# Prompt attention: the third head's near scores on 160 keys per 32 successive queries, and no cache copy behind the 30th weight load

## The chip, the cores and the metric

The kernel runs on one core of one Trainium2 chip. The metric is the time of one execution on the device in microseconds (us), as the median of several runs. A separate execution is profiled; every row shown below comes from that one.

A core has TensorE (PE in the profile; PEld is its loading of weights), VectorE (DVE), ScalarE (ACT), GpSimd (POOL) and SyncE (SP), which here only issues DMAs. Each engine works off its own list of instructions in order, and semaphores tie the lists together. Matmul results arrive in PSUM; everything else lies in SBUF or in HBM.

## The reference

One layer of a decoder is computed for a prompt of 256 tokens and for 8 x 4 sample tokens that share the weights. The part that matters here is the attention of the prompt:

```python
GROUPS = ((128, 1), (512, 4), (2048, 16))     # window, dilation
...
valid = (du >= 0) & (du <= BAND) & (uk >= 0)
bias = slopes[:, None, None] * (dil * du).astype(jnp.float32)[None]
sc = jnp.einsum('nrbqhd,nrbkhd->nrbhqk', qb, kw).astype(jnp.float32) * ATT_SCALE - bias
sc = jnp.where(valid[None, None, :, None], sc, -jnp.inf)
m = jnp.max(sc, axis=-1, keepdims=True)
p = jnp.exp(sc - m)
den = jnp.sum(p, axis=-1, keepdims=True)
```

There are four heads in each of three groups. In group 0 (dilation 1, "near") a query sees its own key and the 128 before it. In groups 1 and 2 (dilations 4 and 16, "far") it sees every fourth or sixteenth key. The three groups' results of a head are merged by their softmax denominators, which comes to one softmax over the scores of all three groups. Around this stand a combined input projection, a gated convolution, an output projection, a feed-forward block with a convolution, and two layer norms; and the caches of the sample tokens are copied from inputs to outputs.

## The kernel before, in words

**Weight blocks.** All dense work is a list of 313 blocks of weights (`weight_list`), each of 128 output features by up to 2048 inputs, behind three blocks that are handled apart. `prepare` (from L196) loads a block into a tile `wst` (three buffers) with a DMA on SyncE's queue, and splits each half of it into a high part `whi` (ScalarE copies, L265) and the rest `wlo` (VectorE subtracts, L265); there are four buffers of halves. `product` takes a block and runs three matmuls for each 128 inputs: `whi` by the high part of x, `whi` by its rest, `wlo` by the high part. Behind the loads with numbers from 20 on that end in 0, 3 or 7, `prepare` calls `copy_rest`, which issues one DMA of the list `copies`: 84 copies of a megabyte from HBM to HBM, the sample caches on their way to the outputs (L163). The list is used from its end, one copy at each such load, so a skipped place shifts all later copies to the next places.

**Order.** The program is written as one sequence, and a planner with a simulated timeline puts each engine's instructions in order before anything runs. `behind` adds an order without a wait; `in_a_row` chains instructions.

**The prompt's attention.** The q blocks come first, then the k and v blocks of the four heads, three of each to a head. Once the third head's are through, `three_heads` (from L579) is started; it is a generator that is advanced behind each following `product`, so that its work lies beside the products of the fourth head. Its steps:

- `score_row` (from L483) issues the score matmuls of three heads in one row, ahead of the next product. For each head, half of the queries (h = 0, 1) and group, four matmuls with 32 queries each (c = 0 to 3) run on the four column strips of TensorE. For the far groups a matmul takes the 32 queries and the keys of one class (positions with the same remainder by 4). For the near group with h = 1 there are two ways, chosen by `in_time(j)`, which is false for `FIRST_HEAD` = 2, the third head, alone:
  - queries in order of time, 32 successive ones to a matmul, which together see only 160 keys (`NB_W`);
  - queries by class, each matmul with all 256 keys.
- The softmax works on rows by class. So scores by time have to be moved: `later_near` (L523) copies them out of PSUM into the tile `by_time`, shifted by 32 columns per strip (four copies of 32x160, on ScalarE, L531), and `by_class_rows` (L533) regroups the rows with four DMAs of SyncE's queue (L537) into the scores' tile `s_half[1]`.
- `softmax(j)` first calls `scored`, six VectorE instructions that add the distance penalties to the scores (L543; the last of them the near group of h = 1, from `s_half[1]` or, for the third head, straight from PSUM), then for each half a maximum, an exponential on ScalarE and a scaling (L554 to L558).
- `weights` transposes the probabilities in blocks of 32 on VectorE (L464) and moves the blocks to their places with ScalarE and GpSimd copies (L472, L468); the ScalarE copies are issued a few to a product, from the list `soon`.
- The heads go in the order third, first, second. With each, the next head's `later_near` is called right after `softmax`, and its `by_class_rows` after `weights`, as there is one `by_time` and one set of `s_half`.

When the fourth head's k and v are through, its own `score_row` also issues `output_row` (from L439, its matmuls L452): the matmuls of the first, second and third head's probabilities with their values, 48 instructions for each head, in that order.

**The penalties.** `load_distances` loads the distances between queries and keys: for h = 0 in four DMAs (one to each class) into one tile `m_first` that holds all groups, for h = 1 in eight, near and far apart.

Of the kernel before, what the change touches and what calls it, by code (L numbers as in the profile page):

```python
# [17 lines left out]
P = 128  # L18
# [35 lines left out]
FIRST_HEAD = 2  # L54
# [34 lines left out]
N_LATE = 3  # L89
N_PAUSE = 5  # L90
# [19 lines left out]
def layer_kernel(ctx: ExitStack, tc: tile.TileContext, ins, outs):  # L110
# [85 lines left out]
    def prepare():  # L196
# [13 lines left out]
        if n >= 20 and n % 10 in (0, 3, 7):  # L210
            copy_rest(d)
# [151 lines left out]
    m_first = pa_take(NG * P).rearrange("p (g k) -> p g k", g=NG)  # L363
    m_near = [m_first[:, 0], pa_take(2 * P)]
    m_all = [m_first[:, 1:], pa_take((NG - 1) * 2 * P).rearrange("p (g k) -> p g k", g=NG - 1)]
# [34 lines left out]
    def load_distances(h):  # L400
# [3 lines left out]
        for c in range(NC):  # L404
            at = slice(c * NW, (c + 1) * NW)
            if h:
                behind(sp.dma_start(m_near[h][at], m[c, :, 0]), w_load[0])
                behind(sp.dma_start(m_all[h][at], m[c, :, 1:]), w_load[0])
            else:
                behind(sp.dma_start(m_first[at], m[c]), w_load[0])  # L410
# [69 lines left out]
    def in_time(j):  # L480
        return j != FIRST_HEAD

    def score_row(heads):  # L483
# [5 lines left out]
        for n, (j, kT, k_class) in enumerate(heads):  # L489
# [49 lines left out]
    def scored(j, s3):  # L539
        s = s_half  # L540
        for h, g in ((0, 0), (0, 1), (0, 2), (1, 1), (1, 2), (1, 0)):
# [3 lines left out]
                s[h][:, at] if h and not g and in_time(j) else s3[h][g],  # L545
# [3 lines left out]
    def softmax(j, s3):  # L549
        s = s_half  # L550
        scored(j, s3)
        for h in range(2):
            st = sb(wk, [P, 4], "st", bufs=4)
            dve.reduce_max(st[:, 0:1], s[h], AX.X)  # L554
            dve.tensor_scalar_mul(st[:, 1:2], st[:, 0:1], -SCALE)
            act.activation(s[h], s[h], AF.Exp, bias=st[:, 1:2], scale=SCALE, accum_out=st[:, 2:3])
            dve.reciprocal(st[:, 3:4], st[:, 2:3])
            dve.tensor_scalar_mul(s[h], s[h], st[:, 3:4])  # L558
# [20 lines left out]
    def three_heads(heads, vT):  # L579
# [935 lines left out]
```

## Time and profile before

| what | value |
|---|---|
| median of 3 runs | 1701.38 us (1700.85 to 1701.54) |
| the profiled execution | 1701.37 us, of which its span is 1699.6 us |
| granted clock of TensorE in it | 0.999 |
| VectorE busy in the span | 1200.9 us |
| SyncE's queue (q1) | 430.54 MB, 69.2% of 16 DMA engines' span |
| row of score matmuls of three heads | 181.9 to 184.8 us |
| row of score and output matmuls with the fourth head | 221.0 to 225.3 us |

How to read the rows below. Times are us from the start of the span, unless marked ns. A row of the timeline is: start, duration (of all that is merged in the row), engine, line of the kernel, operation, written tile <- read tiles, shape, how many; in brackets the idle time of the engine just before, and what ended it. A row of the waits is: who waited <- for whom, us in total, times, longest. A row of the windows is: the stretch, its length, then for PE, PEld, DVE, ACT and POOL the busy time and (x) the number of instructions, then the granted clock, the share of the DMA engines and GB/s. "issue" is a wait for nothing that the profile shows. The matmuls in f32 that belong to the scores are two instructions each; a row of 8 is a set of four.

### The profile page before, as it was taken

The page shows a single profiled execution, that of the slowest core. Times are in us where ns is not written, and L with a number is a line of the kernel's source. Part 1 is how long each engine was busy: PE and PEld are TensorE (multiplying, and loading weights), DVE is VectorE, ACT ScalarE, POOL GpSimd, SP SyncE. Part 2 cuts the span into 40 slices and gives each one's busy share as a digit, 9 for nine tenths or more (in the row PEclk, how much of TensorE's full clock was granted, in tenths as well). Part 3 has the DMA queues.
Part 4 walks back from the last instruction along what each step waited for, and adds up shares of the span by engine and source line. Part 5 has one row for each costly group of instructions (what it writes and reads, how often), then busy time and mean ns, then how long its engine had stood idle before and what let it go on. Part 6 is the DMA issues. An engine that isn't in the chain of part 4 may idle for free.

```text
span 1699.6 us, 34341 instructions
## 1 busy us (share of the span) xinstructions
PE 1692.0 (100%) x14094; PEld 1689.4 (99%) x14094; DVE 1200.9 (71%) x1553; ACT 944.9 (56%) x1694; POOL 396.2 (23%) x529
## 2 busy tenths in 40 slices
PE   9999999999999999999999999999999999999998
PEld 9999999999999999999999999999999999999998
DVE  6477789889887767655888886776554555555576
ACT  6477796665666655544546664555433454445455
POOL 0123232223332221110454440111100010011175
PEclk9999999999999999999999999999999999999999
DMA  9788778676678888577766668666666666767553
GB/s 322 265 304 347 281 285 321 241 251 245 250 293 314 336 303 337 210 261 255 282 236 223 223 216 322 224 255 226 229 239 224 223 228 246 294 223 251 199 174 112
DMA packets 61918, 436.57 MB, mean 257 GB/s; under 512 B 8064, under 2 KB 12288, under 8 KB 24064
## 3 DMA queue, kind: packets, MB, share of 16 engines
q1 hardware_dynamic: 60464, 430.54, 69.2%
q10 hardware_dynamic: 1296, 3.83, 0.6%
q8 instruction: 110, 1.80, 0.4%
q14 instruction: 48, 0.39, 0.1%
HBM read 427.50 MB, written 94.53 MB: 307 GB/s over the span
## 4 chain that ended last, share of the span: by engine, by line
PE 99%; DVE 0%; DMA 0%; issue 0%; ACT 0%; ACTq 0%; DVEq 0%
PE acc L259 32%; PE acc L261 32%; PE acc L260 32%; PE acc L344 1%; PE acc L452 0%; DMA yah<-in_x 0%; DVE acc L1186 0%; PE att L507 0%; PE acc L507 0%; DVE yah L1186 0%; PE acc L1175 0%; PE acc L1172 0%; PE acc L1171 0%; PE att L1090 0%; ACT yah L1196 0%
## 5 line engine op out<-in xcount | busy, mean ns | idle before, releaser
L265 DVE TENSOR_TENSOR wlo<-wst,whi 128x1024 fp32r<-128x1024 f32 (+1 forms) x579 | 746.6, 1292 | 388.0 <-ACT whi L265 383.7
L265 ACT CAST whi<-wst 128x1024 fp32r<-128x1024 f32 (+1 forms) x579 | 588.8, 1020 | 648.9 <-PE acc L260 578.8
L261 PE MATMUL acc<-xh,wlo 128*128 128x288 f32 (+1 forms) x3216 | 920.0, 286 | 0.6 <-issue 0.6
L259 PE MATMUL acc<-xh,whi 128*128 128x288 f32 (+1 forms) x3216 | 920.3, 286 | 0.0
L260 PE MATMUL acc<-xl,whi 128*128 128x288 f32 (+1 forms) x3216 | 920.0, 286 | 0.0
L259 PEld LDWEIGHTS acc<-xh,whi 128*128 128x128 f32 x3216 | 607.8, 189 | 1.2 <-issue 1.1
L260 PEld LDWEIGHTS acc<-xl,whi 128*128 128x128 f32 x3216 | 607.8, 189 | 0.0
L261 PEld LDWEIGHTS acc<-xh,wlo 128*128 128x128 f32 x3216 | 607.8, 189 | 0.0
L260 PE MATMUL acc<-yal,whi 128*128 128x288 f32 x1216 | 347.5, 286 | 0.0
L261 PE MATMUL acc<-yah,wlo 128*128 128x288 f32 x1216 | 347.4, 286 | 0.0
L259 PE MATMUL acc<-yah,whi 128*128 128x288 f32 x1216 | 347.2, 286 | 0.0
L260 PEld LDWEIGHTS acc<-yal,whi 128*128 128x128 f32 x1216 | 229.8, 189 | 0.0
L261 PEld LDWEIGHTS acc<-yah,wlo 128*128 128x128 f32 x1216 | 229.7, 189 | 0.0
L259 PEld LDWEIGHTS acc<-yah,whi 128*128 128x128 f32 x1216 | 229.6, 189 | 0.0
L955 POOL COPY qk_s<-u 128x2 f32<-128x2 f32 x44 | 37.2, 845 | 534.5 <-ACT u L1274 487.1
L943 DVE SCALAR_TENSOR_TENSOR cy<-u,prm,cy 128x304 f32<-128x304 f32 x120 | 71.1, 593 | 6.2 <-ACT cy L941 3.5
L656 POOL TENSOR_TENSOR cache<-cache,cst 128x1024 f32<-128x1024 f32 x16 | 35.4, 2216 | 109.4 <-DMA cache<-in_cv 103.6
L656 POOL TENSOR_TENSOR cache<-cache,qk_s 128x1024 f32<-128x1024 f32 x16 | 32.9, 2058 | 66.1 <-DMA cache<-in_ck 56.5
L966 DVE TENSOR_TENSOR ya<-cy,acc 128x256 f32<-128x256 f32 x104 | 27.7, 310 | 26.6 <-PE acc L261 26.0
L265 ACT CAST yah<-ya 128x288 fp32r<-128x288 f32 x76 | 32.6, 429 | 22.6 <-DVE ya L966 13.6
L654 ACT ACTIVATE cache<-cache,qk_s 128x128 f32<-128x128 f32 x128 | 40.6, 393 | 0.0
L654 ACT ACTIVATE cache<-cache,cst 128x128 f32<-128x128 f32 x128 | 40.0, 391 | 0.0
(288 smaller groups left out, 1187.5 us busy)
## 6 DMA issues: line engine op xcount, KB each, us to landing
wst<-in_w_in SPq DMA_DIRECT2D x112, 1024.0 KB, 5.2
wst<-in_w_up SPq DMA_DIRECT2D x88, 1024.0 KB, 4.9
cache<-in_ck SPq DMA_DIRECT2D x18, 1024.0 KB, 8.0
cache<-in_cv SPq DMA_DIRECT2D x18, 1024.0 KB, 7.7
wst<-in_w_a SPq DMA_DIRECT2D x16, 1024.0 KB, 5.0
wst<-in_w_out SPq DMA_DIRECT2D x16, 1024.0 KB, 4.9
wst<-in_w_down SPq DMA_DIRECT2D x32, 512.0 KB, 4.5
wst<-in_w_down SPq DMA_DIRECT2D x16, 1024.0 KB, 4.8
```

What stands on the lines that cost most here:

```text
L259: pe.matmul(out, hi[:, c, :], xh_k, start=k == 0, stop=False)
L260: pe.matmul(out, hi[:, c, :], xl_k, start=False, stop=False)
L261: last_mm[0] = pe.matmul(out, lo[:, c, :], xh_k, start=False, stop=k == nk - 1)
L265: return act.copy(hi, src), dve.tensor_tensor(lo, src, f32(hi), ALU.subtract)
L344: i = pe.matmul(o[b], first_w(term == 2, b, k), xk, start=k == 0 and term == 0, stop=k == KD - 1 and term == 2,)
L654: behind(act.activation(o[:, a, b], t[:, a, b], AF.Copy, scale=w[:, a, b : b + 1]), w_split[0])
L656: behind(pool.tensor_tensor(o, t, w.unsqueeze(3).broadcast_to([P, *n]), ALU.mult), w_split[1])
L943: dve.scalar_tensor_tensor(y, u[:, i : i + YW], prm[:, w0 + i : w0 + i + 1], y, ALU.mult, ALU.add)
L955: pool.tensor_copy(dst[:, 0:2], u[:, SEQ : SEQ + 2])
L966: dve.tensor_tensor(a, b, c, ALU.mult)
```

## The change

It has three parts.

1. The third head's near scores of h = 1 are computed by time, as the other heads' are: `in_time` goes, all heads take 160 keys per 32 successive queries. The third head's q of the near group is therefore copied in two pieces instead of one. The scores go the way of `later_near` and `by_class_rows`.
2. The order in `three_heads` follows from that. `scored` and `softmax` are split: `EARLY` are the scores that are there without regrouping (h = 0, and the far groups of h = 1), `LATE` is the near group of h = 1; `softmax(h)` does one half. The third head's `later_near` and `by_class_rows` are called right behind `score_row`; its early scores and first half follow, and its late scores and second half come one product later, ahead of `weights`. The first head's `later_near` is called after the third head's `weights`, and no longer beside its softmax.
3. `prepare` leaves out the copy behind load 30 (`N_SCORES`). The distances of h = 0 are loaded like those of h = 1, near and far in tiles of their own, with eight DMAs.

```diff
-FIRST_HEAD = 2
+EARLY, LATE = ((0, 0), (0, 1), (0, 2), (1, 1), (1, 2)), ((1, 0),)
...
+N_SCORES = 30
...
-        if n >= 20 and n % 10 in (0, 3, 7):
+        if n >= 20 and n % 10 in (0, 3, 7) and n != N_SCORES:
             copy_rest(d)
...
-    m_first = pa_take(NG * P).rearrange("p (g k) -> p g k", g=NG)
-    m_near = [m_first[:, 0], pa_take(2 * P)]
-    m_all = [m_first[:, 1:], pa_take((NG - 1) * 2 * P).rearrange("p (g k) -> p g k", g=NG - 1)]
+    m_near = [pa_take((1 + h) * P) for h in range(2)]
+    m_all = [pa_take((NG - 1) * (1 + h) * P).rearrange("p (g k) -> p g k", g=NG - 1) for h in range(2)]
...
-            if h:
-                behind(sp.dma_start(m_near[h][at], m[c, :, 0]), w_load[0])
-                behind(sp.dma_start(m_all[h][at], m[c, :, 1:]), w_load[0])
-            else:
-                behind(sp.dma_start(m_first[at], m[c]), w_load[0])
+            behind(sp.dma_start(m_near[h][at], m[c, :, 0]), w_load[0])
+            behind(sp.dma_start(m_all[h][at], m[c, :, 1:]), w_load[0])
...
-                [second[:, far_keys(1, g) if g else slice(0, NB_W if in_time(j) else 2 * P)] for g in range(NG)],
+                [second[:, far_keys(1, g) if g else slice(0, NB_W)] for g in range(NG)],
...
-                        elif h and in_time(j):
+                        elif h:
                             k = kT[:, c * NW : c * NW + NB_W]
                         else:
-                            k = kT[:, : (1 + h) * P]
+                            k = kT[:, :P]
...
-    def scored(j, s3):
+    def scored(j, s3, parts):
         s = s_half
-        for h, g in ((0, 0), (0, 1), (0, 2), (1, 1), (1, 2), (1, 0)):
+        for h, g in parts:
...
-        order = FIRST_HEAD, 0, 1
+        order = 2, 0, 1
+        later_near(s3[order[0]])
+        by_class_rows()
         for n, j in enumerate(order):
-            softmax(j, s3[j])
-            if n < 2:
-                later_near(s3[order[n + 1]])
+            scored(j, s3[j], EARLY)
+            softmax(0)
+            if n:
+                scored(j, s3[j], LATE)
+                softmax(1)
+            if n == 1:
+                later_near(s3[order[2]])
             yield 1
+            if n == 0:
+                scored(j, s3[j], LATE)
+                softmax(1)
             weights(p_three[j])
+            if n == 0:
+                later_near(s3[order[1]])
             no_keys()
             if n < 2:
                 by_class_rows()
...
-        softmax(head[0], s3[0])
+        scored(head[0], s3[0], EARLY + LATE)
+        softmax(0)
+        softmax(1)
...
-            n = SEQ if g or not in_time(j) else P
+            n = SEQ if g else P
```

More of the change, by code (lines that the diff above doesn't have):

```diff
@@ L478, in moved @@
                 move((a, b), out[b : b + 32, :, a : a + 32], src[a : a + 32, :, b : b + 32], on_dve)
-    def in_time(j):
-        return j != FIRST_HEAD
     def score_row(heads):
@@ L544, in scored, with softmax @@
                 s[h][:, at], m_far[:, h, g - 1, : (1 + h) * NW] if g else m_near[h], -SLOPE[g][j] / SCALE,
-                s[h][:, at] if h and not g and in_time(j) else s3[h][g],
+                s[h][:, at] if h and not g else s3[h][g],
                 ALU.mult, ALU.add,
             )
-    def softmax(j, s3):
+    def softmax(h):
         s = s_half
[L551 to L558, printed above, removed]
+        st = sb(wk, [P, 4], "st", bufs=4)
+        dve.reduce_max(st[:, 0:1], s[h], AX.X)
+        dve.tensor_scalar_mul(st[:, 1:2], st[:, 0:1], -SCALE)
+        act.activation(s[h], s[h], AF.Exp, bias=st[:, 1:2], scale=SCALE, accum_out=st[:, 2:3])
+        dve.reciprocal(st[:, 3:4], st[:, 2:3])
+        dve.tensor_scalar_mul(s[h], s[h], st[:, 3:4])
     def values(vT):
```

## The prediction

> **What bounds the kernel now.** I read the page first, for the share of each engine and for the number of instruction pages.
>
> ```profile
> span 1699.6 us, 34341 instructions
> PE 1692.0 (100%) x14094; PEld 1689.4 (99%) x14094; DVE 1200.9 (71%) x1553; ACT 944.9 (56%) x1694; POOL 396.2 (23%) x529
> ...
> q8 instruction: 110, 1.80, 0.4%
> ```
>
> TensorE is busy for 1692.0 of 1699.6 us; no other engine comes near. So an edit can win time only by taking work from TensorE or by closing one of its gaps, and it can lose time only by opening a gap. I therefore asked next what TensorE waits for, in the view of waits filtered to it, which has these three lines and no more:
>
> ```profile
> PE acc L275 <- PEq L1502: 0.8, 1, 0.8
> PE acc L344 <- ACT xh L316: 0.7, 1, 0.7
> PE acc L261 <- issue: 0.6, 1, 0.6
> ```
>
> The first two are the start of the kernel, before anything that is edited. The third is the only stall in the body. The timeline of TensorE has it at 188.3 us, 3.5 us behind the row of score matmuls that the change edits:
>
> ```profile
> 188.16 0.29 PE L259 MATMUL acc<-xh,whi 128*128 128x288 f32 x1
> 188.28 0.29 PE L260 MATMUL acc<-xl,whi 128*128 128x288 f32 x1
> 189.17 0.28 PE L261 MATMUL acc<-xh,wlo 128*128 128x288 f32 x1 [0.60 <-issue]
> ```
>
> Two matmuls that otherwise follow each other by 0.12 us (188.16 and 188.28) are 0.89 us apart, so the stall costs 0.77 us. "issue" says that no semaphore that the profile knows ended it. The stretches around it, and two answers of the DMA view (for 173.3 to 188.3 us and for 186.4 to 188.3 us), suggest a cause:
>
> ```profile
> 173.00:181.90 8.90, 8.90 (x74) 8.78 (x72) 5.17 (x5) 5.94 (x13) 0.44 (x1) 1.00 0.95 333
> 181.90:184.80 2.90, 2.90 (x146) 2.58 (x145) 2.09 (x4) 2.40 (x6) 1.70 (x5) 1.00 1.01 411
> 184.80:188.30 3.50, 3.50 (x32) 3.50 (x30) 2.94 (x13) 0.89 (x4) 1.37 (x4) 1.00 1.01 413
> ```
>
> ```profile
> q8 instruction: 1, 0.02, 0.5%
> ```
>
> ```profile
> q8 instruction: 1, 0.02, 3.6%
> ```
>
> TensorE runs 2 x 14094 = 28188 instructions and queue 8 carries 110 packets: 256 instructions to a packet, so queue 8 is TensorE's program. Between 173 and 188.3 us TensorE used 146 + 291 + 62 = 499 instructions, nearly two packets' worth, because the score row alone takes 291 in 2.9 us. In that time only one packet came, and it came after 186.4 us. At the usual pace of one packet per 256 instructions it was due when 256 - 146 = 110 of the row's 291 instructions were through, at about 183 us. So the program itself was about 3.5 us late, while the DMA engines were fully taken (shares 0.95, 1.01 and 1.01 in the rows). That the stall is this late packet is my reading; no row names it.
>
> **The change, part by part.** (1) The third head's near scores of the second half: four matmuls of 256 columns become four of 160. The timeline has both shapes:
>
> ```profile
> 183.13 0.46 PE L507 MATMUL long<-dd,yah 128*32 128x160 f32 x8
> 183.41 0.41 PE L507 MATMUL long<-cy,yah 128*32 128x64 f32 x16
> ...
> 183.97 0.62 PE L507 MATMUL acc<-dd,yah 128*32 128x256 f32 x8
> 184.41 0.41 PE L507 MATMUL acc<-yal,yah 128*32 128x64 f32 x16
> ```
>
> From start to start the 160-column group takes 0.28 us and the 256-column group 0.44 us. The change takes 0.16 us from TensorE and leaves its number of instructions as it is.
>
> (2) The copy behind load 30 goes. In the trace it is this one (behind it on the same queue a cache load and the next weight loads; rows of SyncE's DMA lines with their time to landing):
>
> ```profile
> L163 SPq DMA_DIRECT2D out_o_ck<-in_ck x1: 793/793/793, 172.9 to 172.9; - x1
> ...
> DMA to landing us min/median/max: 9.5/9.5/9.5
> ```
>
> ```profile
> L821 SPq DMA_DIRECT2D cache<-in_ck x1: 531/531/531, 173.8 to 173.8; - x1
> ...
> DMA to landing us min/median/max: 12.2/12.2/12.2
> ```
>
> The copy lands at 172.9 + 9.5 = 182.4, the cache load at 173.8 + 12.2 = 186.0: the queue is served in order, at about 3.6 us a megabyte here. The late packet of instructions started just behind that landing. Without the copy the cache load lands near 182.4 and everything behind it some 3 to 3.6 us sooner, so at 183 us one transfer less stands ahead of the packet. To spare TensorE the stall it must come 0.77 us sooner. Bounds for this term: nothing (the packet is as late as now) and 0.77 us (the stall is gone). I take 0.77, since 3 us of backlog vanish where 0.8 are needed.
>
> The list of copies is only shifted, so one more copy runs at the end, behind load 300 at about 1606 us. It is a megabyte like the others, and the weights behind it have time:
>
> ```profile
> wst<-in_w_down SPq DMA_DIRECT2D x16, 768.0 KB, 4.4
> ```
>
> ```profile
> 1611.29 54.91 SPq L207 DMA_DIRECT2D wst<-in_w_down  x13
> ```
>
> ```profile
> 1622.73 1.05 ACT L265 CAST whi<-wst 128x1024 fp32r<-128x1024 f32 x1
> ```
>
> The load issued at 1611.29 is first read at 1622.73, 11.4 us later, and such loads land after 4.4 us (the DMA view's row). A whole 3.6 us of copy ahead of it still fits. I cost it at nothing; without that cover it would be at most 3.6 us.
>
> (3) The distances of the first half come in eight DMAs, not four, and the q copy of the third head is two ScalarE copies of 128 columns, not one of 256. Four more issues of 0.41 us (row below) hold SyncE's queue for 1.6 us at 27 us, ahead of a weight load; the q copy adds one ScalarE instruction, of some 0.3 us by the copies in part 4 (1.21 us for four). TensorE shows no wait there now, so nothing; the bound is 1.6 us, if that load were already the last thing that TensorE waits for.
>
> ```profile
> L410 SPq DMA_DIRECT2D yal<-in_cst x4: 382/410/421, 26.0 to 27.3; - x4
> ```
>
> (4) The third head, which is first in the softmax order, now takes the way of the others: four ScalarE copies to the buffer by time, four DMAs that regroup it by class, and only then the last scores and the second softmax. The rows of these in before (ScalarE, VectorE, SyncE, and the chain that ended last):
>
> ```profile
> 183.67 1.21 ACT L531 COPY yal<-att 32x160 f32<-32x160 f32 x4 [0.41 <-ACT dd L910]
> ...
> 191.57 1.05 ACT L265 CAST whi<-wst 128x1024 fp32r<-128x1024 f32 x1 [1.95 <-PE acc L260]
> ...
> 219.79 1.32 ACT L472 COPY yah<-yah 32x160 f32<-32x160 f32 x4
> ```
>
> ```profile
> 189.37 0.85 DVE L464 STREAM_TRANSPOSE yah<-yal 128x640 f32<-128x640 f32 x1
> ...
> 195.34 0.42 DVE L543 SCALAR_TENSOR_TENSOR yal<-yal 128x256 f32<-128x256 f32 x1 [1.13 <-DMA yal<-yal]
> ...
> 204.89 0.84 DVE L464 STREAM_TRANSPOSE yah<-yal 128x640 f32<-128x640 f32 x1
> ...
> 210.05 0.43 DVE L543 SCALAR_TENSOR_TENSOR yal<-yal 128x256 f32<-128x256 f32 x1
> ...
> 214.39 0.85 DVE L464 STREAM_TRANSPOSE yah<-yal 128x640 f32<-128x640 f32 x1
> ```
>
> ```profile
> 190.29 3.72 SPq L537 DMA_DIRECT2D yal<-yal  x4
> 194.11 0.53 SPq L207 DMA_DIRECT2D wst<-in_w_in  x1
> 194.69 0.56 SPq L163 DMA_DIRECT2D out_o_cv<-in_cv  x1
> ```
>
> ```profile
> 222.04 3.29 PE acc L452 x144
> ```
>
> The four copies cost ScalarE 1.21 us, the DMAs 3.72 us of SyncE's queue at a time (185 to 190 us) in which it has nothing else to issue. Scores are done at about 184.4, copied at 185.7, and then the four DMAs: now it takes from their first issue at 190.29 to the last scores at 195.34, 5.1 us, so the third head's last scores start at 185.7 + 5.1 = 190.8. From the last scores to the end of the transposition the second head needs 210.05 to 215.24, 5.2 us. So its transposition ends at 190.8 + 5.2 = 196.0 and not at 190.2: 5.8 us later. The next head's regrouping starts from there, and with 5.1 us more its last scores start at 201.1. If the load and the copy of 194.11 and 194.69 stand in front, it is up to 202.6. So the last scores of the first head come 5.8 to 7.3 us late. But between those scores and the end of that head's transposition pass now 10.4 us (195.34 to 205.73) where the bare chain needs 5.2; VectorE fills the rest with moves of values that can as well run while it waits. So 0.6 to 2.1 us of lateness are left for the second head, whose last moves end at 219.79 + 1.32 = 221.1 now, and then at 221.7 to 223.2.
>
> Who waits for them is TensorE's output row at 222.04, of 3.29 us for three heads, one after the other: the second head's weights are read from 222.04 + 1.1 = 223.1, and with TensorE 0.9 us ahead of now from 222.2. So the chain ends between 0.5 us ahead of its time and 1.0 us behind it. Bounds: nothing below (this chain cannot give TensorE anything), and 7.3 - 1.1 = 6.2 us above, if VectorE's other work does not move into the wait. I take nothing, the end at which the count without the copy in front arrives; the rest is the second rival.
>
> **Sum.** 0.16 from the columns and 0.77 from the stall, nothing from the rest: 0.93 us less. The profiled execution took 1701.37 us (1699.6 of span and 1.8 around it), the median is 1701.38, so the two need no correction: 1701.4 - 0.9 = 1700.5 us, 0.05% faster, which is no change by the measure of 0.2% (3.4 us), about what a measurement of this kernel can tell from no change.
>
> **Rivals.** *The stall stays.* The packet of instructions comes as late as now, because the loads that move up take the place of the copy: DMA shares stay near 1.0 until 188 us. For it: three more megabytes stand in the queue. Against it: 3 us less ahead of the packet. Time: 1701.37 - 0.16 = 1701.2 us. A page of the Trainium skill would have it so: "DMA: Bandwidth & Descriptors", section "Queues, rings and completion order", says that each DMA engine goes round its queues packet by packet, so that a fetch on its own queue would not stand behind whole transfers of another. The landing at 186.0 and the fetch just after it speak against it, though not for certain. "Runtime: NRT & Kernel Launch", section "Instruction fetch mechanics", has programs fetched in blocks of 256 instructions, as counted here, but gives TensorE room for 2048; with that much, 499 instructions could not starve it, and the stall would be something else and stay. By either rule the sum is 1701.2.
>
> *The regrouping comes late and TensorE waits at its output row* (the slower side). The mechanism is the chain of part 4: one more DMA round trip ahead of two others, with the copy of 194.69 in front of the second. It decides from about 1.1 us of lateness at the second head's last moves (222.2 - 221.1). Price: lateness less 1.1 us; at 2 us of lateness it takes back the gain (1701.3), at 4 us it is 1703.3, at the full 7.3 us 1706.6. For it: by the count above there is hardly any slack. Against it: the 5.2 us of other work in that chain, which the count moves only as far as the wait is long.
>
> *Weights come late* because VectorE, waiting in order for a DMA, holds back a weight rest: it needs a wait of more than 2 us more than now at one place. ScalarE's casts in this stretch wait for TensorE to free a buffer (1.95 us at 191.57), so the weights are ahead. Price: what the wait exceeds 2 us by; 1702 to 1704 us for 1.5 to 3.5 us.
>
> **How the numbers follow.** Forecast (columns and stall) 0.45; stall stays 0.2; late regrouping 0.27, of which 0.05 beyond 3.4 us; late weights 0.06; anything faster by over 3.4 us 0.02, since only 7.6 us of the span are not TensorE's, most of them at its two ends. Range: from 1700.0, the forecast less half the spread of the runs, to 1703.0, which takes in the stall that stays and the late regrouping up to 3.6 us of lateness; beyond it stand about 0.15. Faster by over 0.2%: 0.02; within: 0.92; slower: 0.06.
>
> **What would show it.** Right: the group of the third head's near matmuls is 0.28 us long; no "issue" line near 188 us, and queue 8's packet before 185.9 us; the cache load of 173 us lands near 182.4; no wait of TensorE at the output row (L452 in before). Wrong: a gap of TensorE at 222 us that ends on ScalarE, GpSimd or a transposition; a gap between 185 and 221 us that ends on a weight rest; a stall "issue" as long as before.

## The result and the profile after

| | before | after |
|---|---|---|
| median (8 runs each, side by side) | 1701.31 us (1700.75 to 1701.54) | 1705.72 us (1704.04 to 1707.27) |
| ratio after : before | | 1.0026, 95% interval 1.0017 to 1.0036 |
| the profiled execution, its span | 1701.37, 1699.6 us | 1704.78, 1703.0 us |

The changed kernel is slower by 4.4 us in the medians and by 3.4 us in the two profiled executions (the profile before has a stall of 0.77 us in it that not every execution has, as the last experiment shows). That lies outside the predicted range (1700.0 to 1703.0). The second rival came true, and a part of the third with it.

The view of waits, filtered to TensorE, of the kernel after (who waited <- for whom, us in total, times, longest):

```profile
PE acc L449 <- ACT yah L469: 2.8, 1, 2.8
PE acc L262 <- DVE wlo L266: 0.9, 1, 0.9
PE acc L276 <- PEq L1507: 0.8, 1, 0.8
```

The third line was there before. The "issue" line is gone, as predicted; the first two lines are new. TensorE's timeline shows where they are (start, duration, line, tiles, form; in brackets the idle time before the row and what ended it):

```profile
183.16 0.46 PE L501 MATMUL long<-dd,yah 128*32 128x160 f32 x8
183.43 0.41 PE L501 MATMUL long<-cy,yah 128*32 128x64 f32 x16
...
184.00 0.46 PE L501 MATMUL acc<-dd,yah 128*32 128x160 f32 x8
184.27 0.41 PE L501 MATMUL acc<-yal,yah 128*32 128x64 f32 x16
...
220.98 1.28 PE L449 MATMUL acc<-yah,yal 128*32 128x256 f32 x48
225.08 1.30 PE L449 MATMUL acc<-yah,yal 128*32 128x256 f32 x48 [2.82 <-ACT yah L469]
...
251.16 0.29 PE L261 MATMUL acc<-xl,whi 128*128 128x288 f32 x1
252.31 0.39 PE L262 MATMUL acc<-xh,wlo 128*128 128x288 f32 x1 [0.87 <-DVE wlo L266]
```

The third head's near group takes 0.27 us from start to start (184.00 to 184.27) where it took 0.44. But the output row stops between the first head's 48 matmuls and the second head's: these start at 225.08, where 222.1 was due (220.98 and the 1.1 us that 48 matmuls take). The last matmul before the gap starts at 221.99, so the gap is 3.09 us from start to start; the same step took 0.09 us before (222.86 to 222.95). The matmul at 252.31 comes 1.15 us after its neighbour, 1.03 too late, and the next one 0.11 more (at 252.54).

The bookkeeping from the start of the score row (181.93 before, 181.95 after) to the last matmul (1693.61 and 1696.91), in us: columns -0.16, stall at 188.3 -0.77, wait in the output row +3.00, the rest of the row of the fourth head's scores and the outputs +0.05, weight rest +1.14: +3.26. Measured: 1511.68 us before, 1514.96 after, +3.28. (The first output matmul starts at 221.85 in before, 39.92 us behind the score row; the prediction's 222.04 is where the chain view begins to count that row.)

Behind the wait stand VectorE, ScalarE and SyncE's queue (the timeline of each; compare the transpositions at 189.37, 204.89 and 214.39 before):

```profile
192.35 0.42 DVE L537 SCALAR_TENSOR_TENSOR yal<-yal 128x256 f32<-128x256 f32 x1 [2.32 <-DMA yal<-yal]
...
196.43 0.85 DVE L461 STREAM_TRANSPOSE yah<-yal 128x640 f32<-128x640 f32 x1
...
203.12 2.90 DVE L467 COPY yah<-yal 32x192 f32<-32x192 f32 x11
...
206.14 0.40 DVE L537 SCALAR_TENSOR_TENSOR yal<-yal 128x256 f32<-128x256 f32 x1
...
210.31 0.85 DVE L461 STREAM_TRANSPOSE yah<-yal 128x640 f32<-128x640 f32 x1
...
220.06 0.85 DVE L461 STREAM_TRANSPOSE yah<-yal 128x640 f32<-128x640 f32 x1
```

```profile
184.80 1.21 ACT L525 COPY yal<-acc 32x160 f32<-32x160 f32 x4 [1.52 <-PE acc L501]
...
222.62 2.32 ACT L469 COPY yah<-yah 32x160 f32<-32x160 f32 x7
```

```profile
178.38 6.21 SPq L208 DMA_DIRECT2D wst<-in_w_in  x2
186.03 2.45 SPq L531 DMA_DIRECT2D yal<-yal  x4
195.89 0.33 SPq L208 DMA_DIRECT2D wst<-in_w_in  x1
196.27 0.56 SPq L164 DMA_DIRECT2D out_o_ck<-in_ck  x1
197.30 2.41 SPq L531 DMA_DIRECT2D yal<-yal  x4
```

| what | before | after | later by |
|---|---|---|---|
| third head's transposition, start | 189.37 | 196.43 | 7.06 |
| first head's, start | 204.89 | 210.31 | 5.42 |
| second head's, start | 214.39 | 220.06 | 5.67 |
| second head's last ScalarE move, end | 221.11 | 224.94 | 3.83 |

The copies at 203.12 are the moves of the third head's values: `values` transposes them, `moved` puts the blocks in their places, with 12 copies on VectorE. So 7.06 us of lateness came in with the third head, and 3.83 us of it reached the moves that the output row waits for. The predicted price was lateness less 1.1 us: 2.7 us; the trace has 2.82.

### The profile page after: what moved, and what is told of

The parts are those of the page before. It is cut to its first block, busy times and chain, and to the rows that moved or that the text cites. A ratio compares the mean times of both kernels' runs of the same rounds, so it can differ in the third digit from the quotient of the medians.

```text
span 1703.0 us, 34360 instructions
## 1 busy us (share of the span) xinstructions
PE 1692.9 (99%) x14094; PEld 1690.2 (99%) x14094; DVE 1198.9 (70%) x1553; ACT 946.1 (56%) x1699; POOL 396.7 (23%) x529
## 3 DMA queue, kind: packets, MB, share of 16 engines
q10 hardware_dynamic: 1296, 3.83, 0.6%
## 4 chain that ended last, share of the span: by engine, by line
PE 97%; DMA 1%; ACT 1%; DVE 0%; issue 0%; SPq 0%; ACTq 0%; DVEq 0%
PE acc L262 32%; PE acc L260 32%; PE acc L261 32%; PE acc L345 1%; DMA out_o_k<-dd 1%; DMA yal<-yal 0%; PE acc L276 0%; ACT whi L266 0%; DVE wlo L266 0%; ACT cache L659 0%; ACT dd L469 0%; PE att L501 0%; PE acc L1180 0%; PE acc L1177 0%; PE acc L1176 0%
```

## The experiments

All ratios are to the kernel before on the same chip. Its median was 1701.21 us beside the two runs with the copy behind load 30, the one with a transfer less and the one with the output row later; 1700.96 beside the third head from PSUM, the detour alone, the values early and the first head's regrouping early; 1701.13 beside the last three versions. The intervals reach about 0.1% (1.7 us) to each side, so differences of under 2 us between two versions are read from the traces here and not from the medians.

### Which part costs the time

**The copy alone.** The kernel before, without the copy behind load 30:

```diff
-        if n >= 20 and n % 10 in (0, 3, 7):
+        if n >= 20 and n % 10 in (0, 3, 7) and n != 30:
```

> The kernel before, with only the copy behind load 30 left out. Theory (the stall of 0.77 us near 188 us is the late packet of TensorE's program, held up by the DMA backlog): the line 'issue' near 188 us is gone, queue 8's packet starts before 185.9 us, no new wait: 1700.5 us. Rival (the stall has another cause, and in the changed kernel it went with the new order): the stall stays, 1701.3 us.

Measured: 1701.13 us (1700.66 to 1701.33), ratio 0.9997 (0.9988 to 1.0006). In its trace the stall is gone, and from the score row's start to the last matmul 0.8 us are gone too; in the medians 0.1 us is left, so the time is nearer to the rival's than to the theory's. Why, is taken up with the last experiment.

**The copy put back.** The kernel after, with the copy behind load 30:

```diff
-        if n >= 20 and n % 10 in (0, 3, 7) and n != N_SCORES:
+        if n >= 20 and n % 10 in (0, 3, 7):
```

> The changed kernel with the copy behind load 30 kept. Theory (the regrouping DMAs wait in SyncE's queue behind what was issued before them): the third head's regrouping lands about 3 us later than at 192.2 us, the output row's wait of 2.8 us grows by 1 to 3 us, and the stall of 0.8 us near 188 us is back: 1707 to 1710 us. Rival (the chain is as long as it is, whatever lies in the queue): only the 0.8 us come back, 1706.5 us.

Measured: 1706.54 us (1705.68 to 1708.03), ratio 1.0029 (1.0019 to 1.0040). Two lines of TensorE's waits:

```profile
PE acc L449 <- ACT yah L469: 2.8, 1, 2.8
...
PE acc L262 <- issue: 0.5, 1, 0.5
```

The stall is back, and the wait at the output row is the same to 0.01 us (2.82), as the rival had it. The third head's regrouping lands at 192.6 to 193.5 us instead of 191.8 to 192.2, not 3 us later. So the copy has nothing to do with that wait.

**The third head straight from PSUM again**, the rest of the diff kept (order, distances, copy):

```diff
-                [second[:, far_keys(1, g) if g else slice(0, NB_W)] for g in range(NG)],
+                [second[:, far_keys(1, g) if g else slice(0, NB_W if j != 2 else 2 * P)] for g in range(NG)],
...
-                        elif h:
+                        elif h and j != 2:
...
-                            k = kT[:, :P]
+                            k = kT[:, : (1 + h) * P]
...
-                s[h][:, at] if h and not g else s3[h][g],
+                s[h][:, at] if h and not g and j != 2 else s3[h][g],
...
-        later_near(s3[order[0]])
-        by_class_rows()
...
-            n = SEQ if g else P
+            n = SEQ if g or j == 2 else P
```

> The changed kernel with the third head's near scores by class and on 256 columns again, read straight from PSUM; the split softmax, the order of calls, the distances' DMAs and the missing copy stay. Theory (the third head's own regrouping makes its transposition 7 us late, and everything behind it is a chain of the engines' orders with too little room): that transposition starts near 190 us, no wait at the output row, 1700.4 to 1701.4 us. Rival (the new order of calls, the first head's copies behind the third head's weights above all, costs the time): 1703 us or more.

Measured: 1701.40 us (1700.99 to 1701.85), ratio 1.0002 (0.9992 to 1.0011), and no wait of TensorE behind the start of the kernel. The whole loss is gone.

**The third head's detour alone**, put into the kernel before:

```diff
     def in_time(j):
-        return j != FIRST_HEAD
+        return True
...
+        later_near(s3[order[0]])
+        by_class_rows()
         for n, j in enumerate(order):
```

> The kernel before with only the third head's near scores changed: 160 keys by time, copies and regrouping right behind the score row, the rest of the order of calls and the copy behind load 30 as before. Theory: its transposition starts near 197 us, the output row waits 2 to 3.5 us, 1705 to 1707 us, as the changed kernel with the copy kept. Rival (order of calls): within 1 us of before, 1701 to 1702 us.

Measured: 1705.78 us (1705.27 to 1706.45), ratio 1.0029 (1.0017 to 1.0041). The longest of TensorE's waits:

```profile
PE acc L452 <- ACT yah L472: 2.8, 1, 2.8
```

The detour (four ScalarE copies, four DMAs, the wait for them) is by itself the whole loss; the split of `softmax`, the distances and the copy are none of it.

### Why the chain didn't take the lateness in

**A transfer less in front of the second regrouping.** The kernel after, without the copy behind load 33 too (issued at 196.27, just ahead of the regrouping of 197.30):

```diff
-        if n >= 20 and n % 10 in (0, 3, 7) and n != N_SCORES:
+        if n >= 20 and n % 10 in (0, 3, 7) and n not in (N_SCORES, 33):
```

> The changed kernel with the copy behind load 33 left out as well; the planner then puts the first head's late scores ahead of 11 of the 12 moves of values. Theory (the copy in front of the first head's regrouping and the moves in front of its late scores make the chain late): that regrouping lands near 201.8 us instead of 204.4, its late scores start near 202 instead of 206.1, and the output row waits 0 to 0.8 us instead of 2.8: 1701.0 to 1702.5 us. Rival (the extra regrouping alone makes the chain too long): the wait stays over 2 us, 1704.5 to 1706 us.

Measured: 1705.06 us (1703.86 to 1706.90), ratio 1.0023 (1.0013 to 1.0032). My theory at that point, that SyncE's queue sets the chain, fell. The DMA view (tile, KB each, median us from issue to landing) for this regrouping, after and without the copy:

```profile
yal<-yal SPq DMA_DIRECT2D x4, 32.0 KB, 5.8
```

```profile
yal<-yal SPq DMA_DIRECT2D x4, 32.0 KB, 3.3
```

VectorE's timeline without the copy:

```profile
197.19 0.84 DVE L461 STREAM_TRANSPOSE yah<-yal 128x640 f32<-128x640 f32 x1
...
203.78 0.41 DVE L537 SCALAR_TENSOR_TENSOR yal<-yal 128x256 f32<-128x256 f32 x1
...
210.94 0.84 DVE L461 STREAM_TRANSPOSE yah<-yal 128x640 f32<-128x640 f32 x1
```

The DMAs take 2.5 us less, the first head's late scores follow the third head's transposition by 6.6 us instead of 9.7, and yet from transposition to transposition it is 13.75 us instead of 13.88, and the wait stays at 2.81. The late scores now stand ahead of 11 of the 12 moves of values and not behind them; the stretch is as long either way. Something other than the landing sets these 13.9 us.

**The output row one product later:**

```diff
-        if o_next:
-            some_moves(len(soon))
-            row += output_row()
         in_a_row(row)
...
         values(vT)
+        yield 1
+        some_moves(len(soon))
+        in_a_row([last_mm[0]] + output_row())
         moved(late_v, v_squares)
-        yield 1
```

> The changed kernel with the output row of the first three heads one product (5.9 us) behind the fourth head's scores. Theory (the loss is the deadline of the output row): no wait of TensorE there; the weight rest at 251 us that came 1.0 us late may stay late: 1700.4 to 1701.6 us. Rival (the late chain costs through the late weights, by VectorE's order, not through the output row): the time stays near 1704 us, with waits on weight rests in place of the output row's.

Measured: 1706.17 us (1705.64 to 1706.90), ratio 1.0028 (1.0017 to 1.0038). Its waits of TensorE, without those at the start of the kernel:

```profile
PE acc L262 <- DVE wlo L266: 1.2, 1, 1.2
PE acc L261 <- issue: 1.1, 1, 1.1
...
PE acc L260 <- ACT whi L266: 0.4, 1, 0.4
```

No wait is left in the output row, but the time isn't won: a weight half and a rest come late at 252.5 and 254.2 us, and an "issue" stall stands at 235.5, behind the row. VectorE and ScalarE are late as such, not only for that one row. The stall is a loss of its own: it costs 1.29 us, ends 2.25 us behind a packet of queue 8 (233.26), and so looks like the one at 188 us; its place, too, fits (last experiment).

**What sets the 13.9 us.** The windows between the third and the first head's transposition (stretch, length, then PE, PEld, DVE, ACT and POOL busy; granted clock, DMA share, GB/s), before, before without the copy, and after (with the stretch ahead of it):

```profile
189.37:204.89 15.52, 15.52 (x129) 15.52 (x128) 11.60 (x32) 12.29 (x28) 2.33 (x5) 1.00 0.56 200
```

```profile
189.58:204.35 14.77, 14.77 (x123) 14.77 (x122) 11.67 (x32) 12.28 (x28) 3.22 (x5) 1.00 0.55 200
```

```profile
196.43:210.31 13.88, 13.88 (x115) 13.88 (x114) 11.68 (x31) 11.39 (x28) 2.42 (x5) 1.00 0.68 237
...
188.81:196.43 7.62, 7.62 (x64) 7.62 (x64) 4.08 (x8) 3.98 (x9) 0.00 (x0) 1.00 0.07 23
```

VectorE works 11.6 to 11.7 us between the two transpositions, before as after. So at most 15.52 - 11.60 = 3.9 us could be taken in there, and 1.6 were. Of both, 0.77 us is the stall at 188.3, which lies in that stretch of the first profile: without it (second row) it is 14.77 us long, the room is 3.1 us and 0.9 were taken in. Meanwhile in the stretch ahead, where the third head waits, VectorE is busy for 4.08 of 7.62 us: there the moves of values would fit, but their place in VectorE's list is behind it (203.12 in the timeline above). One experiment moves this work out of the full stretch, a second takes the first head's copies and DMAs out of it.

**The values' work called right behind the third head's regrouping:**

```diff
         by_class_rows()
+        values(vT)
+        moved(v_three[2], v_squares, True)
         for n, j in enumerate(order):
...
-            if n == 0:
-                values(vT)
-                moved(v_three[2], v_squares, True)
```

> The changed kernel with the third head's values transposed and moved ahead of its late scores, so that VectorE's 12 moves (3.2 us) fall into the wait for the first regrouping and no longer between the third and the first head's transpositions. Theory (chain of engine orders): the 13.0 us from the third to the first head's transposition become about 10, the output row waits at most 0.5 us, 1701 to 1702.5 us. Rival (the chain is bound by DMA landings): the first head's late scores wait for their landing as before, the output row's wait stays over 2 us, 1704.5 to 1706 us.

Measured: 1703.79 us (1702.21 to 1707.67), ratio 1.0021 (1.0011 to 1.0031). TensorE's waits, without those at the start of the kernel:

```profile
PE acc L449 <- ACT yah L469: 1.4, 1, 1.4
PE acc L262 <- DVE wlo L266: 1.0, 1, 1.0
```

The theory's 10 us and 0.5 us of wait were not reached, nor the rival's 2 us. The window between the transpositions, and how long VectorE is busy in it:

```profile
196.91:209.30 12.39, 12.39 (x103) 12.39 (x103) 8.94 (x19) 11.13 (x28) 2.42 (x5) 1.00 0.77 266
```

VectorE has 2.7 us less to do there, but the stretch is only 1.5 us shorter: the first head's late scores, at 205.05, now wait 0.57 us for their DMAs.

**The first head's copies and regrouping ahead of the third head's weights**, into a tile of their own:

```diff
+    near_rows = sb(big, [P, 2 * P], "near_rows")
...
-            behind(sp.dma_start(s_half[1][at, : 2 * P], by_time[c::NC]), w_load[0])
+            behind(sp.dma_start(near_rows[at], by_time[c::NC]), w_load[0])
...
-                s[h][:, at] if h and not g else s3[h][g],
+                near_rows if h and not g else s3[h][g],
...
-            weights(p_three[j])
             if n == 0:
                 later_near(s3[order[1]])
-            no_keys()
             if n < 2:
                 by_class_rows()
+            weights(p_three[j])
+            no_keys()
```

> The changed kernel with a tile of its own for the regrouped rows, so that a head's regrouping need not wait for the transposition of the head before; the first head's copies and regrouping are called ahead of the third head's weights. Theory (chain): the first head's regrouping is issued near 194 us instead of 197.3, its late scores start before 200 us instead of at 206.1, the output row waits 0 to 0.5 us, 1700.5 to 1702 us. Rival (VectorE has too little room in this stretch for any order with the detour): the lateness shows up as waits on weight rests, 1703.5 us or more.

Measured: 1703.87 us (1703.34 to 1705.25), ratio 1.0017 (1.0008 to 1.0027). TensorE's waits, without those at the start of the kernel:

```profile
PE acc L449 <- ACT yah L469: 1.6, 1, 1.6
PE acc L262 <- DVE wlo L266: 0.8, 1, 0.8
```

The window between the transpositions:

```profile
196.35:209.95 13.60, 13.60 (x113) 13.60 (x112) 11.48 (x31) 11.18 (x28) 2.52 (x5) 1.00 0.68 245
```

The regrouping is issued at 193.49 and the first head's late scores start at 197.90 instead of 206.14, as the theory said; but the stretch is nearly as long as ever, and the wait did not go. With 11.48 us of work left in VectorE's list, scores that are there 8 us sooner help little. What is won comes one head later (8.28 us from the first to the second head's transposition, 9.75 after).

Each takes 1.2 to 1.4 us out of the wait. From the row's start to the last matmul they are 1.4 and 1.1 us below after (1513.54 and 1513.86 to 1514.96). The medians are 1.9 us below the 1705.72 of after, which the intervals don't tell from nothing.

### Whether the loss can be taken back

**The third head's regrouping ahead of the weight load** that was issued just before it (the second load of the row at 178.38):

```diff
+    regrouped = []
...
+        if n == 32:
+            behind(d, regrouped[3])
...
-            behind(sp.dma_start(s_half[1][at, : 2 * P], by_time[c::NC]), w_load[0])
+            regrouped.append(sp.dma_start(s_half[1][at, : 2 * P], by_time[c::NC]))
+            behind(regrouped[-1], w_load[0])
```

> The changed kernel, with the third head's four regroup DMAs issued ahead of the weight load that stood in front of them at 184.3 us; nothing else is moved. Theory (a chain of fixed orders that absorbs about 2 us in all): the DMAs are issued at about 186 us as before but land within some 3 us, at 188.5 to 189.5 instead of 192.2; the third head's late scores start near 190 instead of 192.35, and its transposition 2 us sooner, at about 194.4 instead of 196.4. The wait at the output row falls by as much, from 2.8 to 0.5 to 1.2 us, and the time from 1705.7 to about 1703.8. Rival (the cast of 193.6 us on ScalarE, which stands ahead of the exponential, sets the chain, not the landing): the late scores come sooner, the exponential does not, the transposition stays at 196.4 and the wait at 2.8 us, time 1705.5. Second rival (the weight load, now behind the four DMAs, comes late): a wait of TensorE on a weight half between 188 and 200 us of 0.5 to 2 us.

Measured: 1703.73 us (1703.19 to 1704.49), ratio 1.0014 (1.0004 to 1.0024). The median came as the theory said, but not by its mechanism, so the agreement proves nothing: the wait is 2.3 us, not 0.5 to 1.2, and of the 2.0 us between the medians the trace shows 0.3 from the row's start to the last matmul (1514.62 us). The rest stays open; the profiled run, 1704.49 us, is the slowest of this kernel's. Three of the DMAs landed by 189.1, the fourth, issued at 187.82, only at 191.63; no run here shows what held it. VectorE's timeline:

```profile
191.76 0.43 DVE L541 SCALAR_TENSOR_TENSOR yal<-yal 128x256 f32<-128x256 f32 x1 [1.80 <-DMA yal<-yal]
...
195.83 0.84 DVE L464 STREAM_TRANSPOSE yah<-yal 128x640 f32<-128x640 f32 x1
...
209.71 0.84 DVE L464 STREAM_TRANSPOSE yah<-yal 128x640 f32<-128x640 f32 x1
```

The late scores start 0.6 us sooner, the transposition too, and the wait is 0.5 us shorter: what the third head is late goes nearly whole into the wait. The stretch between the transpositions is 13.88 us again, to the hundredth.

**The values early and the first head's regrouping early, together:**

> The changed kernel with both of the edits that each took 1.2 to 1.4 us from the wait at the output row: the values' transposes and moves called right behind the third head's regrouping, and the first head's copies and regrouping ahead of the third head's weights, into a tile of its own. Theory (each takes its own piece out of one chain): the pieces add, 2.8 less 1.4 less 1.2, 0.2 us are left at the output row; the wait for a weight rest at 250 us stays at 0.5 to 1 us; time about 1702.5. Rival (both take the same piece, the wait of VectorE ahead of the first head's late scores): the wait at the output row stays at 1.3 to 1.6 us and the time at 1703.8.

Measured: 1702.31 us (1701.21 to 1703.98), ratio 1.0007 (0.9998 to 1.0017). The stretch from the third head's transposition to the first's, and from there to the second's:

```profile
196.70:206.16 9.46, 9.46 (x80) 9.46 (x79) 6.58 (x18) 8.48 (x24) 2.52 (x5) 1.00 0.75 262
206.16:215.62 9.46, 9.46 (x79) 9.46 (x79) 8.50 (x19) 9.22 (x24) 3.49 (x5) 1.00 0.53 200
```

Together they do more than the sum of each alone in the first stretch: 9.46 us instead of 13.88, where one alone left 12.4 and the other 13.6. Alone, the first still had to wait for the DMAs of the regrouping, and the second still had all of VectorE's work in the stretch. There is no wait in the output row (0.2 us were expected), though the third head is as late as after the change (196.70). That makes the full stretch behind it, not the landing of its DMAs, the place where most of the loss arose. What is left is a wait of 1.48 us for a weight rest at 250.7, longer than the 0.5 to 1 us expected.

**All three together:**

> The changed kernel with all three edits: the third head's regroup DMAs ahead of the weight load, the values' work called early, the first head's regrouping ahead of the third head's weights. Theory: no wait at the output row is left; the work of VectorE and ScalarE behind it is 2 to 4 us sooner, so that the wait for a weight rest at 250 us goes too; what remains against before is the gain of 0.16 us and whatever the stall at 188 us was worth, time 1700.5 to 1701.3, the same as before within 0.05%. Rival (the extra eight instructions of the detour fill ScalarE and the queue anyway, and the loss only moves to the last head's weights): the wait at 250 us stays at 0.8 us or grows, time 1702 to 1703.

Measured: 1701.21 us (1700.86 to 1701.83), ratio 1.0000 (0.9991 to 1.0010). VectorE's timeline:

```profile
190.92 0.42 DVE L543 SCALAR_TENSOR_TENSOR yal<-yal,near_rows 128x256 f32<-128x256 f32 x1
...
194.99 0.84 DVE L464 STREAM_TRANSPOSE yah<-yal 128x640 f32<-128x640 f32 x1
...
204.45 0.84 DVE L464 STREAM_TRANSPOSE yah<-yal 128x640 f32<-128x640 f32 x1
...
213.92 0.84 DVE L464 STREAM_TRANSPOSE yah<-yal 128x640 f32<-128x640 f32 x1 [0.20 <-ACT yah L472]
```

The third head is still 5.6 us later than before (194.99 to 189.37), and TensorE waits nowhere in the body. The last transposition starts 31.70 us behind the score row's start, as in before without the copy (31.69). From the row's start to the last matmul it takes 1510.75 us, 0.16 less than the 1510.91 of before without the copy: the gain of the columns, and nothing lost. The detour as such can be hidden. But nothing is won by it either: no version here beats the kernel before by what a measurement can tell.

### Whether the stall at 188 us is always there

**The kernel before, unchanged, with a second profile:**

> The kernel before, unchanged, with a second profile. Theory (the stall at 188.3 us is there in each execution, and the gain of b_no30 in the medians is hidden by the start of the kernel, which varies by some 0.5 us): the line of a wait for 'issue' of 0.5 to 0.7 us is there again at 3.5 us behind the score row, and from the row's start to the last matmul it takes 1511.6 to 1511.9 us as in the first profile (181.93 to 1693.61). Rival (the late packet is chance, there in some executions only): no such line, and 0.7 us less between the same two marks.

Measured: 1701.5 us, one run. TensorE's waits are all from the start of the kernel:

```profile
PE acc L344 <- ACT yal L311: 0.9, 1, 0.9
PE acc L275 <- PEq L1502: 0.8, 1, 0.8
PE acc L344 <- ACT xh L316: 0.4, 1, 0.4
```

No stall: the rival is right, and from the row's start to the last matmul it takes 1510.91 us, 0.77 less than in the first profile and exactly as much as without the copy. Against these two the kernel after (1514.96) is 4.05 us longer, which is nearer to the 4.4 us of the medians. But the theory's other half holds too. Here the score row starts 0.9 us later (182.83), because of a longer wait at the start, and yet the last matmul starts only 0.13 us later (1693.74) than in the first profile. The packets of queue 8, put beside the row's start in each trace, show how:

| kernel | copy behind load 30 | row starts | packet | packet after row's start | stall |
|---|---|---|---|---|---|
| before | yes | 181.93 | 186.63 | 4.70 | 0.77 |
| after, copy put back | yes | 182.09 | 186.67 | 4.58 | 0.65 |
| before, detour alone | yes | 182.08 | 186.24 | 4.16 | none |
| before, second profile | yes | 182.83 | 186.87 | 4.04 | none |
| before, without the copy | no | 182.15 | 183.71 | 1.56 | none |
| after | no | 181.95 | 184.05 | 2.10 | none |

With the copy the packet comes at 186.2 to 186.9, without it at 183.7 to 185.7 in the ten traces that have none (185.6 with the regrouping ahead of the load, 185.7 with the output row later, where the score row itself starts at 183.91). In the table TensorE stalls where the packet comes more than 4.2 to 4.6 us behind the row's start. It resumes 2.4 to 2.5 us after the packet; in the detour alone it passes the same place 2.16 us after one without a stop. That these stalls are the program coming late is borne out by their place: they come behind 1629 matmuls of the whole execution in both cases here and behind 2141 in the version with the output row later. The difference, 512 matmuls or 1024 instructions, is four times 256, so all three stand at the same place of a packet's 256 instructions.

So the stall ends at a time that the packet sets: of the two executions of before, the one that started its row early waited here and the one that started late didn't, and the stall took back most of what the early start had won. The start alone doesn't decide it (182.08 without a stall, 182.09 with one), as the packet's time varies too. That fits the 0.1 us in the medians; how many executions stall isn't known, since only profiled ones show it.

## Why the prediction was wrong

**(1) The columns: right.** 0.16 us, as predicted. What it brought with it is part 4.

**(2) The copy: the mechanism right, the size not.** The cache load of 173.7 us lands after 7.4 us, so at 181.1 (predicted: near 182.4), the packet comes 2.6 us sooner, and the "issue" line is gone. My reading of the stall as a late packet of TensorE's program stands up in six traces, and by the place of the three stalls among the 256 instructions of a packet. What failed is the step "no correction" between profile and median: the 0.77 us belonged to that execution; the copy alone is worth 0.1 us of median, by that run's interval no more than 2.0. By the Trainium skill, "DMA: Bandwidth & Descriptors", "Queues, rings and completion order", a DMA engine goes round its queues packet by packet, so that the copy shouldn't have mattered to a fetch on another queue; the traces speak against that use of it (a megabyte less, and the packet 2.6 us earlier), though none tells when the fetch was asked for. The extra copy at the end, and part (3), cost nothing that a wait of TensorE shows.

**(4) The detour: the step that failed is the 5.2 us that the chain was to take in.** The first half of the count was near: the third head's late scores were due at 190.8 and came at 192.35, since a weight load issued at 184.27 stood ahead of the four DMAs in SyncE's queue and landed at 191.6, just before them (the prediction counted what SyncE issues from 185 on, not what was still under way; with the load behind them three of the four landed by 189.1), and its transposition was 7.06 us late where 5.8 were predicted.

Then the prediction subtracted 10.4 - 5.2 = 5.2 us from the first head's stretch, on the ground that VectorE's other work "can as well run while it waits". That work didn't go away; it changed sides. From the first head's late scores to the end of its transposition it is 5.0 us after (206.14 to 211.16), close to the predicted 5.2, but the moves of values and the other work now stand ahead of these scores, which start at 206.14 and not at 201.1 to 202.6. The count asked for 10.3 to 11.8 us from the third head's transposition to the first's, with 11.6 us of VectorE's own work in between; it took 13.88. Nor could the work run in the new wait by itself: each engine goes through its list in order, and the moves of values stood behind the late scores of the third head. VectorE idled 2.32 us in that wait and then did the same 11.7 us of work in the next stretch. Against the first profile 1.64 us were taken in there, 0.9 if the stall that lay in it is left out, and 1.8 at the second head's last moves.

That this is the cause is shown from both sides: with the values moved into the wait and the first head's regrouping early the stretch is 9.46 us and the output row doesn't wait; with DMAs sooner and VectorE's work left where it was it is 13.60 to 13.88, and the row waits.

**The rivals.** The late regrouping came true with its own price, lateness less 1.1 us; it had 0.27, mostly for less than 3.4 us, because of the same wrong 5.2. The weights that come late weren't an alternative to it but its second half: VectorE's and ScalarE's work behind the output row is late by the same chain, and one weight rest at 251 us costs 1.1 us more. That the stall stays was wrong in the trace and near the truth in the medians. The second rule named for it, by which 499 instructions could not starve TensorE, does not fit: three stalls stand at the same place of a packet's 256 instructions, each 2.25 to 2.54 us behind a packet.

**The signs named:** a gap at 222 us that ends on a ScalarE move of probabilities was the first sign for "wrong", and it is the first line of the waits. The gap on a weight rest was named for the stretch from 185 to 221 us; it came at 251.

## What to carry to other kernels

Before lateness in a chain is written off against "other work" in it, look where that work stands in its engine's list: work that stands behind the waiting instruction can't fill the wait, and a stretch can shrink by its engine's idle time at most (14.8 - 11.7 us here), not by all that isn't the chain's own. Where two things keep a stretch long, taking away either alone shows little of what both are worth. Here a new round trip by DMA became cheap only when work was put into its wait by hand, the next round trip was brought forward, and no large load was issued just ahead of it on its queue. And a stall that one profile shows should be looked for in a second profile of the same kernel before it is counted as a gain.

## What the hardware showed unexpectedly

- TensorE's own program came late in three of 14 traces: after a row of 291 instructions in 2.9 us (twice), or behind the later output row (once), it stood still until 2.25 to 2.54 us behind a packet of queue 8. The three places are the same modulo 256 instructions.
- A megabyte copied on another queue moved that packet, counted from the row's start, by 3.1 us (before, with and without the copy) and 2.5 us (after, with and without it).
- The stall's end is set by the packet and not by the start of the execution: in the two profiles of before the score row started 0.9 us apart and the last matmul 0.13 us.
- Four DMAs of 32 KB from SBUF to SBUF landed after a median of 2.5 us when issued 6.0 us behind a weight load of a megabyte (before, at 190.29), and of 5.0 us when issued 1.8 us behind one (after, at 186.03). The DMA view of both:

```profile
yal<-yal SPq DMA_DIRECT2D x4, 32.0 KB, 2.5
```

```profile
yal<-yal SPq DMA_DIRECT2D x4, 32.0 KB, 5.0
```
